# A two-layer float32 encoder on one core: x and the result kept with features on the partitions, and the first gate and up products alternating chunk by chunk

## The chip, the core and the metric

The kernel runs on one core of one Trainium2 chip. The metric is the device time of one execution in microseconds (us), taken as the median of 3 runs. Lower is better.

## The reference

An encoder of two layers works on x of 512 tokens by 1024 features, in float32. Each layer does three things:

- `x = x + 0.5 * swiglu(rms_norm(x))` with gate and up weights of 1024 x 2816 and a down weight of 2816 x 1024;
- `x = x + heads(rms_norm(x) @ w_in) @ w_out`, with four groups of attention heads;
- a second `x = x + 0.5 * swiglu(rms_norm(x))` with weights of its own.

`swiglu(h)` is `(silu(h @ w_gate) * (h @ w_up)) @ w_down`. The output is x after the second layer.

## The kernel before

TensorE multiplies float32 in halves: every operand is split into `hi` (rounded) and `lo` (the rest), and `mm3` (L237 to L240) issues three matmuls, hi by hi, hi by lo and lo by hi. ScalarE (ACT) makes `hi` as a cast on L190, VectorE (DVE) or GpSimd (POOL) makes `lo` on L191.

The residual stream lies on chip as eight tiles X[0..7], each of 128 features on the partitions by 512 tokens. XH and XL are its halves, scaled by the norm's gain. The norm's factor per token is not applied to them: products are made from the unscaled stream, and the factor R, spread over all partitions, multiplies each gate and up result when it leaves PSUM (L321, L325). So a gate product can begin before the sum of squares is known. The squares go through ACT and POOL into `acc`; `token_rstd` (L278) sums them on TensorE (L283), and `spread` (L294) makes R with one more matmul (L300).

A feed-forward block (`ffn`, L286) works on 22 column blocks of 128 in four groups (6, 6, 6 and 4). For a pair of columns the gate product (`wi` 0) and the up product (`wi` 1) each run over eight chunks of features, into two PSUM banks each. That is 8 chunks x 2 column blocks x 3 = 48 matmuls of 512 columns for the gate and 48 for the up. Then the down products of the group follow.

Weights come in blocks of 4 chunks by 256 columns (512 KB) through SP's DMA queue into three buffers `raw`, and are split two chunks at a time (a "piece") up to four pieces ahead of use (`run`, L193).

**The start.** x lies in memory as tokens by features, in the order of a 64-wide grid, while the kernel keeps tokens in blocks of 16 grid columns. So x comes in eight transfers `xin` (L849; four blocks of tokens, two halves of the features), each with a source of 8 x 16 rows of 2 KB. For each of the eight chunks, `begin` (L853) turns four 128 x 128 squares on TensorE (L867), which gives the chunk in PSUM; ACT makes XH (L868), DVE makes XL (L869) and copies X out (L874). The order of the first steps is written by hand (L412): four chunks, the first gate piece, two chunks, and so on. The gate runs its first four chunks, then the up its first four, then the gate its last four.

**The end.** The last group of the last block uses `row_products` (L368) instead of `down_products`: tokens on the partitions, 256 output columns to a matmul, 4 x 4 x 4 x 3 = 192 matmuls. For that `turn_rows` (L357) turns X back to tokens by features, with 32 more transposes on TensorE (L364) between the last up products. The result leaves in 16 transfers (L386) with a destination of 8 x 16 rows of 1 KB.

The names `psa`, `psb`, `psc` and `pso` are PSUM banks (2, 3, 2 and 1 of them). The order of work on each engine is the order in which the program writes it.

Of the kernel before, what the change touches and what calls it, by code (L numbers as in the profile page):

```python
# [10 lines left out]
F32 = mybir.dt.float32  # L11
# [14 lines left out]
# weight blocks being loaded, pieces of them held as halves, and pieces split ahead of the one in use  # L26
# [26 lines left out]
# those that stay on chip  # L53
# [3 lines left out]
def constants():  # L57
    """Tables and masks that depend on the shapes alone; the masks are for negated scores."""
# [10 lines left out]
    # tokens lie in blocks of 16 grid columns: (block, row, column)  # L69
# [22 lines left out]
    # windows of the grid's columns: row p is (grid row, column p % 16 of a block)  # L92
# [9 lines left out]
# the vectors of one layer that every partition holds: name -> (first column, columns)  # L102
# [21 lines left out]
def weave(mains, fills, ends):  # L124
    """Two streams of steps side by side: the part fills[i] is through when the share ends[i] of mains[i] is."""
# [21 lines left out]
def encoder(ctx: ExitStack, tc: tile.TileContext, a: dict, out: bass.AP):  # L147
# [45 lines left out]
    def run(steps):  # L193
        """Issue the steps, loading the weights and splitting them ahead of their use."""
        pieces = [x.src + (x.aside,) for x in steps if x.src]
        blocks = []
        for b, _, _ in pieces:
            if not blocks or blocks[-1] is not b:
                blocks.append(b)
        raws, ready = {}, []  # L200
        loaded = [0]

        def load(n):
            while loaded[0] < min(n, len(blocks)):
                b = blocks[loaded[0]]
                raw = raws[id(b)] = wp.tile([P, b.shape[1], b.shape[2]], F32, tag="raw", name="raw", bufs=RAW)
                nc.sync.dma_start(out=raw, in_=b)
                loaded[0] += 1

        fetch_x(0)  # L210
        load(1)
        fetch_x(1)
        load(RAW)
        used = at = 0
        for x in steps:
            used += x.src is not None
            while len(ready) < min(len(pieces), used + x.ahead):
                b, k, aside = pieces[len(ready)]
                if b is not blocks[at]:
                    # the block before is split: its place is free for another  # L220
                    at += 1
                    load(at + RAW)
                w = raws[id(b)][:, k:k + 2, :]
                hi, lo = (wp.tile([P, 2, b.shape[2]], F32R, tag=n, name=n, bufs=PIECES) for n in ("hi", "lo"))
                split(w, hi, lo, aside)
                ready.append((hi, lo))
            if x.src:
                x.go(ready[used - 1])
            else:
                x.go()  # L230

    def rows(w, r0, n, c0, m):
        """The pieces of n chunks of 128 rows and m columns: two chunks each."""
        b = w[r0 * P:(r0 + n) * P, c0:c0 + m].rearrange("(c p) f -> p c f", p=P)
        return [(b, k) for k in range(0, n, 2)]
# [6 lines left out]
    def feed(dc, g):  # L242
        """X[dc] is final: its scaled halves for the next products, and its squares."""
# [682 lines left out]
```

## Time and profile before

| | |
|---|---|
| runs | 2103.21, 2104.29, 2105.97 us; median 2104.29 us |
| profiled execution, first to last instruction | 2102.3 us |
| PE busy | 2043.9 us (97%), 10648 matmuls |
| PEld, DVE, ACT, POOL busy | 1689.5, 1067.8, 798.3, 408.1 us |
| read from memory, written | 176.56 MB, 2.10 MB (85 GB/s over the span) |

The profile states no time of its own for the profiled execution beside its span; the median of the runs is 2.0 us longer than the span. PE is TensorE, PEld its loads of the stationary operand, which overlap the matmuls. A matmul's shown duration includes its way through the array, so in a dense stretch the distance between two starts, not the duration, is what a matmul costs.

### The profile page before, as it was taken

Reading aid. Unit: us, or ns where it says so; the run is one execution under the profiler, and the core shown is the slowest. Engines: PE = TensorE matmul, PEld = TensorE weight load, DVE = VectorE, ACT = ScalarE, POOL = GpSimd, SP = SyncE. Lnnn points to the kernel's source line nnn. Section 1 sums busy time; section 2 is a strip of 40 time slices with the busy share of each in tenths; the row PEclk is TensorE's granted clock in tenths of the full one; section 3 lists DMA queues with packets and bytes.
Section 4 is the critical chain, followed back from the end, with each engine's and each line's share of the span. In section 5 each row is a group of like instructions: output and inputs, shape, how many; then the busy total and the mean of one; then the engine's idle time right before and its main releaser. Section 6 shows DMA issues by size and latency. Waiting matters only on the chain. (4 is left out here: it accounts for less than half of the span.)

```text
span 2102.3 us, 27434 instructions
## 1 busy us (share of the span) xinstructions
PE 2043.9 (97%) x10648; PEld 1689.5 (80%) x10648; DVE 1067.8 (51%) x1861; ACT 798.3 (38%) x1576; POOL 408.1 (19%) x403
## 2 busy tenths in 40 slices
PE   7999999999889999999999999999999899999998
PEld 5888888887767888888888888889887578888888
DVE  4444344757566543444454444455675664444444
ACT  4323222556554432332343322235565444232322
POOL 2000001364351200000110000033543511000100
PEclk9999999999989999999999999999999899999999
DMA  4333333321111323333333233333111123323232
GB/s 136 101 100 94 97 98 96 91 69 51 61 31 51 101 91 100 101 91 100 91 98 100 88 106 91 100 94 91 59 41 61 31 62 103 104 82 110 81 111 71
DMA packets 176514, 180.43 MB, mean 86 GB/s; under 512 B 6224, under 2 KB 174288, under 8 KB 176384
## 3 DMA queue, kind: packets, MB, share of 16 engines
q1 hardware_dynamic: 173632, 173.04, 27.5%
q0 software_dynamic: 1376, 4.50, 0.6%
q8 instruction: 83, 1.36, 0.3%
q10 hardware_dynamic: 1376, 1.14, 0.2%
q14 instruction: 47, 0.39, 0.1%
HBM read 176.56 MB, written 2.10 MB: 85 GB/s over the span
## 5 line engine op out<-in xcount | busy, mean ns | idle before, releaser
L190 ACT CAST hi<-raw 128x512 fp32r<-128x512 f32 x648 | 384.7, 618 | 488.3 <-PE pso L239 157.5
L191 DVE TENSOR_TENSOR lo<-raw,hi 128x512 fp32r<-128x512 f32 x566 | 392.5, 724 | 325.8 <-ACT hi L190 325.4
L326 POOL TENSOR_TENSOR u<-g,u 128x512 f32<-128x512 f32 x88 | 111.9, 1292 | 1225.7 <-DVE u L325 1225.7
L238 PE MATMUL psb<-XH,hi 128*128 128x512 f32 x556 | 217.4, 391 | 0.0
L239 PE MATMUL psb<-XL,hi 128*128 128x512 f32 x556 | 216.8, 390 | 0.0
L240 PE MATMUL psb<-XH,lo 128*128 128x512 f32 x556 | 216.8, 390 | 0.0
L191 POOL TENSOR_TENSOR lo<-raw,hi 128x512 fp32r<-128x512 f32 x82 | 112.4, 1380 | 240.6 <-ACT hi L190 236.5
L238 PE MATMUL psa<-hi,XH 128*128 128x256 f32 x512 | 154.8, 302 | 1.6 <-ACT qk L518 1.6
L238 PE MATMUL psa<-XH,hi 128*128 128x512 f32 x392 | 155.4, 396 | 0.0
L239 PE MATMUL psa<-XL,hi 128*128 128x512 f32 x392 | 153.2, 391 | 0.0
L240 PE MATMUL psa<-XH,lo 128*128 128x512 f32 x392 | 153.1, 391 | 0.0
L239 PE MATMUL psa<-lo,XH 128*128 128x256 f32 x512 | 144.4, 282 | 0.0
L240 PE MATMUL psa<-hi,XL 128*128 128x256 f32 x512 | 144.3, 282 | 0.0
L190 ACT CAST ph<-u 128x512 fp32r<-128x512 f32 x88 | 54.7, 622 | 228.5 <-POOL u L326 228.5
L322 ACT ACTIVATE g<-g 128x512 f32<-128x512 f32 x88 | 55.6, 632 | 206.3 <-DVE g L321 204.2
L238 PE MATMUL psc<-XH,hi 128*128 128x512 f32 x328 | 127.6, 389 | 0.0
L239 PE MATMUL psc<-XL,hi 128*128 128x512 f32 x328 | 127.6, 389 | 0.0
L240 PE MATMUL psc<-XH,lo 128*128 128x512 f32 x328 | 127.6, 389 | 0.0
L240 PEld LDWEIGHTS psb<-XH,lo 128*128 128x128 f32 x556 | 104.6, 188 | 21.8
L238 PEld LDWEIGHTS psb<-XH,hi 128*128 128x128 f32 x556 | 104.7, 188 | 21.6
L239 PEld LDWEIGHTS psb<-XL,hi 128*128 128x128 f32 x556 | 104.8, 188 | 21.5
L238 PEld LDWEIGHTS psa<-hi,XH 128*128 128x128 f32 x512 | 97.1, 190 | 23.7 <-issue 17.9
(226 smaller groups left out, 4339.8 us busy)
## 6 DMA issues: line engine op xcount, KB each, us to landing
raw<-in_ffn_w_gate_dram SPq DMA_DIRECT2D x88, 512.0 KB
raw<-in_ffn_w_up_dram SPq DMA_DIRECT2D x88, 512.0 KB
raw<-in_ffn_w_down_dram SPq DMA_DIRECT2D x64, 512.0 KB
raw<-in_w_in_dram SPq DMA_DIRECT2D x44, 512.0 KB
raw<-in_ffn_w_down_dram SPq DMA_DIRECT2D x48, 256.0 KB
raw<-in_w_out_dram SPq DMA_DIRECT2D x16, 512.0 KB
xin<-in_x_dram SPq DMA_DIRECT2D x8, 256.0 KB
dl<-in_consts_dram POOLq DMA_DIRECT2D x8, 256.0 KB, 4.6
```

The costliest lines, as they stand in the source:

```text
L190: nc.scalar.copy(hi, src)
L191: (nc.gpsimd if aside else nc.vector).tensor_tensor(out=lo, in0=src, in1=hi.bitcast(F32), op=ALU.subtract)
L238: nc.tensor.matmul(o, lh, rh, start=start, stop=False, skip_group_check=shared)
L239: nc.tensor.matmul(o, lh, rl, start=False, stop=False, skip_group_check=shared)
L240: nc.tensor.matmul(o, ll, rh, start=False, stop=stop, skip_group_check=shared)
L322: nc.scalar.activation(out=g, in_=g, func=AF.Silu)
L326: nc.gpsimd.tensor_tensor(out=u, in0=st["g", j], in1=u, op=ALU.mult)
```

## The change

The host hands x over as 1024 features by 512 tokens in the kernel's own order of tokens, and turns the result back. In the kernel:

- x comes straight into X, one transfer of 128 x 512 for each chunk. `begin` keeps only XH, XL and the squares, which now read X; the 32 transposes, the eight copies and the identity's own transfer are gone. The constants come in one transfer (POOL's queue, at chunk 5).
- The transfers of x and of the first four weight blocks are cut and interleaved: chunk 0 with gate and up chunk 0, chunk 1 likewise, then chunks by two. One of them goes through ACT's queue. The second and fourth block use buffers of the tag `pt`, which x no longer needs.
- In the first column pair the gate and up products alternate: gate chunk 0, up chunk 0, gate 1, up 1, gate 2 and 3, up 2 and 3, and so on. Their results leave PSUM (`finish_up`) only after `spread`, which now comes in the next pair's gate product.
- The last group uses `down_products` like all others: 96 matmuls of 512 columns. `turn_rows` and `row_products` are gone. The result leaves from X, in transfers of 128 x 512, the last two chunks in halves of 128 x 256.

The diff, cut to its core (blank lines that replace comments are left out):

```diff
-        fetch_x(0)
-        load(1)
-        fetch_x(1)
-        load(RAW)
...
+        firsts = [(b, place(b, ("raw", "pt")[i % 2])) for i, b in enumerate(blocks[:4])]
+        for c0, c1 in ((0, 1), (1, 2), (2, 4), (4, 6), (6, 8)):
+            for c in range(c0, c1):
+                nc.sync.dma_start(out=X[c], in_=a["x"][c * P:(c + 1) * P, :])
+            for i in range(2):
+                b, raw = firsts[2 * (c0 // 4) + i]
+                (nc.scalar if c0 == 0 and i == 0 else nc.sync).dma_start(out=raw[:, c0 % 4:c0 % 4 + c1 - c0, :], in_=b[:, c0 % 4:c0 % 4 + c1 - c0, :])
+        load()
...
-        vps = psum("c")
+        vps = psum("c" if preload else "b")
...
+                if first and fp == 0:
+                    st["late", wi] = lambda banks=st[wi]: finish_up(fp, wi, banks)
+                else:
+                    finish_up(fp, wi, st[wi])
...
+                end = last and final and dp == NDC - 2 and k0 + 2 == nf
+                order = [(k, j) for k in range(2) for j in range(2)]
+                for k, j in sorted(order, key=lambda kj: kj[1]) if end else order:
...
+                        if last and final:
+                            r = slice((dp + j) * P, (dp + j + 1) * P)
+                            for q in (slice(0, 256), slice(256, 512)) if dp == NDC - 2 else (slice(0, 512),):
+                                o = X[dp + j][:, q]
+                                nc.vector.scalar_tensor_tensor(
+                                    out=o, in0=st["d"][j][:, q], scalar=0.5, in1=o, op0=ALU.mult, op1=ALU.add)
+                                (nc.scalar if j else nc.sync).dma_start(out=out[r, q], in_=o)
+                            continue
...
-        def turn_rows(t, hf):
...
-        def row_products(f0, nf, c0, k0, src):
...
+                    if first and fp == 0:
+                        for k, n in ((0, 1), (1, 1), (2, 2)) if kb == 0 else ((0, 2), (2, 2)):
+                            steps += [up_products(fp, wi, kb + k, (src[wi][0][0], k, n)) for wi in range(2)]
...
-            return ([begin(dc) for dc in range(4)] + steps[:1] + [begin(4), begin(5)] + steps[1:2] + [begin(6), begin(7)] + steps[2:4] + [Step(0, rstd)] + steps[4:5] + [Step(0, spread)] + steps[5:])
+            return (b[:1] + steps[:1] + b[1:2] + steps[1:2] + b[2:4] + steps[2:4] + b[4:6] + steps[4:6] + b[6:] + steps[6:11]
+                    + [Step(0, rstd)] + steps[11:12] + [Step(0, spread), late] + steps[12:])
...
         def go():
             gc = gcol[:, 0, dc:dc + 1]
-            pt = psum("b" if dc < 3 else "c")
-            for t in range(4):
-                nc.tensor.transpose(pt[:, t * P:(t + 1) * P], xin[t][:, dc * P:(dc + 1) * P], ident)
-            nc.scalar.activation(out=XH[dc], in_=pt, func=AF.Copy, scale=gc)
...
+            nc.scalar.activation(out=XH[dc], in_=X[dc], func=AF.Copy, scale=gc)
...
+    given["x"] = np.ascontiguousarray(arr["x"][0].reshape(8, 4, 16, D).transpose(3, 1, 0, 2).reshape(D, S))
...
+    out = nc.dram_tensor("out_0_dram", (D, S), F32, kind="ExternalOutput").ap()
```

TensorE's order at the start of the program, before (`xin` are the x transfers' tiles, XH_84 and XH_85 the first two chunks, `hi` and `lo` the weight halves):

```order
L867 MATMUL psb<-cst,xin 128x128 x12
L867 MATMUL psc<-cst,xin 128x128 x4
L238 MATMUL psa<-XH_84,hi 128x512
L239 MATMUL psa<-XL_92,hi 128x512
L240 MATMUL psa<-XH_84,lo 128x512
L238 MATMUL psa<-XH_84,hi 128x512
L239 MATMUL psa<-XL_92,hi 128x512
L240 MATMUL psa<-XH_84,lo 128x512
L238 MATMUL psa<-XH_85,hi 128x512
```

And with the change (psa is the gate, psb the up):

```order
L250 MATMUL psa<-XH_84,hi 128x512
L251 MATMUL psa<-XL_92,hi 128x512
L252 MATMUL psa<-XH_84,lo 128x512
L250 MATMUL psa<-XH_84,hi 128x512
L251 MATMUL psa<-XL_92,hi 128x512
L252 MATMUL psa<-XH_84,lo 128x512
L250 MATMUL psb<-XH_84,hi 128x512
L251 MATMUL psb<-XL_92,hi 128x512
L252 MATMUL psb<-XH_84,lo 128x512
L250 MATMUL psb<-XH_84,hi 128x512
L251 MATMUL psb<-XL_92,hi 128x512
L252 MATMUL psb<-XH_84,lo 128x512
```

Sixteen transposes stood ahead of the first product and sixteen more between products; now the first product is the first instruction, and chunk 0 serves twelve matmuls instead of six before chunk 1 is wanted.

SP's DMA queue at the start, before:

```order
L849 DMA xin<-in_x_dram 128x1x512 x4
L207 DMA raw<-in_ffn_w_gate_dram 128x4x256
L849 DMA xin<-in_x_dram 128x1x512
L849 DMA xin<-in_x_dram 128x1x512 [waits DMAHW0_49]
L849 DMA xin<-in_x_dram 128x1x512 [waits DMAHW1_49]
L849 DMA xin<-in_x_dram 128x1x512 [waits DMAHW2_49]
L207 DMA raw<-in_ffn_w_up_dram 128x4x256 [waits DMAHW3_49]
L207 DMA raw<-in_ffn_w_gate_dram 128x4x256 [waits DMAHW4_49]
```

And with the change (raw_107 is the up block in a `pt` buffer; a DMAHW semaphore is that of an earlier transfer, eight back):

```order
L220 DMA X_76<-in_x_dram 128x512
L223 DMA raw_107<-in_ffn_w_up_dram 128x256
L220 DMA X_77<-in_x_dram 128x512
L223 DMA raw<-in_ffn_w_gate_dram 128x256
L223 DMA raw_107<-in_ffn_w_up_dram 128x256
L220 DMA X_78<-in_x_dram 128x512
L220 DMA X_79<-in_x_dram 128x512 [waits DMAHW0_49]
L223 DMA raw<-in_ffn_w_gate_dram 128x2x256 [waits DMAHW1_49]
L223 DMA raw_107<-in_ffn_w_up_dram 128x2x256 [waits DMAHW2_49]
L220 DMA X_80<-in_x_dram 128x512 [waits DMAHW3_49]
L220 DMA X_81<-in_x_dram 128x512 [waits DMAHW4_49]
L223 DMA raw<-in_ffn_w_gate_dram 128x2x256 [waits DMAHW5_49]
```

Half of all features of every token had to come before the first chunk could be turned; now the first chunk is one transfer, and 17 transfers on SP's queue and one on ACT's carry what 12 carried on SP's.

TensorE's order where the norm's factor is spread, with the change (psc is the second column pair's gate, pso_385 the spread factor, psb_413 and pso_414 the second pair's up; the sums of squares stand twelve matmuls earlier):

```order
L250 MATMUL psc_338<-XH3_87,hi_281 128x512
L251 MATMUL psc_338<-XL3_95,hi_281 128x512
L252 MATMUL psc_338<-XH3_87,lo_282 128x512
L312 MATMUL pso_385<-dg_383,ones_75 128x512
L250 MATMUL psb_413<-XH0_84,hi_299 128x512
L251 MATMUL psb_413<-XL0_92,hi_299 128x512
L252 MATMUL psb_413<-XH0_84,lo_300 128x512
L250 MATMUL pso_414<-XH0_84,hi_299 128x512
```

Before, both stood inside the first pair (after its up product's fourth chunk and its gate product's sixth); now the sums come after the 108th product of the program and the spread after the 120th, and pso_414 waits for ACT to have copied the factor out of pso_385.

## Rows read from the trace of the kernel before

**Rows 1.** The page's first part: span, and busy time, share of the span and instructions of the engines.

```profile
span 2102.3 us, 27434 instructions
PE 2043.9 (97%) x10648; PEld 1689.5 (80%) x10648; DVE 1067.8 (51%) x1861; ACT 798.3 (38%) x1576; POOL 408.1 (19%) x403
```

**Rows 2.** What PE waited for in the whole span: us in total, times, longest us.

```profile
PE psb L867 <- DMA xin<-in_x_dram: 9.5, 4, 5.2
PE psc L867 <- DVE X L874: 2.9, 2, 2.3
PE psc L867 <- DMA xin<-in_x_dram: 1.4, 1, 1.4
```

**Rows 3.** Busy time by stretch, from the start to the 121st gate or up matmul: length, busy us of PE, PEld, DVE, ACT, POOL (instructions), granted clock, share of the DMA engines, GB/s.

```profile
0.00:13.59 13.59, 4.11 (x17) 3.24 (x17) 1.52 (x3) 3.29 (x5) 0.20 (x4) 1.00 0.66 173
13.59:34.43 20.84, 16.52 (x66) 12.77 (x64) 13.56 (x21) 11.81 (x21) 12.98 (x10) 0.92 0.64 180
34.43:52.81 18.38, 18.38 (x84) 14.90 (x83) 9.51 (x17) 8.41 (x15) 2.54 (x2) 1.00 0.20 58
```

**Rows 4.** The timeline of the start: start us, duration us, engine, line, operation, and in brackets the idle time before it and what ended it.

```profile
0.74 2.77 SPq L849 DMA_DIRECT2D xin<-in_x_dram  x4
...
5.16 0.47 PE L867 MATMUL psb<-cst,xin 128*128 128x128 f32 x1 [5.16 <-DMA xin<-in_x_dram]
...
10.90 2.18 PE L867 MATMUL psb<-cst,xin 128*128 128x128 f32 x9 [1.46 <-DMA xin<-in_x_dram]
...
12.27 0.69 ACT L868 ACTIVATE XH<-psb,gcol 128x512 fp32r<-128x512 f32 x1 [0.17 <-PE psb L867]
...
12.85 0.62 ACT L190 CAST hi<-raw 128x512 fp32r<-128x512 f32 x1
...
13.59 0.78 PE L238 MATMUL psa<-XH,hi 128*128 128x512 f32 x1
...
17.04 0.40 PE L240 MATMUL psa<-XH,lo 128*128 128x512 f32 x1
...
20.10 0.77 PE L867 MATMUL psc<-cst,xin 128*128 128x128 f32 x5 [1.41 <-DMA xin<-in_x_dram]
...
20.94 0.40 PE L239 MATMUL psa<-XL,hi 128*128 128x512 f32 x1
...
22.75 0.62 ACT L190 CAST hi<-raw 128x512 fp32r<-128x512 f32 x1 [0.29 <-DMA raw<-in_ffn_w_gate_dram]
...
27.85 0.78 PE L238 MATMUL psb<-XH,hi 128*128 128x512 f32 x1
...
30.55 0.40 PE L238 MATMUL psb<-XH,hi 128*128 128x512 f32 x1
...
52.81 0.39 PE L238 MATMUL psb<-XH,hi 128*128 128x512 f32 x1
...
54.17 0.39 PE L238 MATMUL psb<-XH,hi 128*128 128x512 f32 x1
```

**Rows 5.** The timeline around the norm's factor: the last product ahead of the sums of squares and the first behind them, the products around the spread (L300), and ACT's copy of it.

```profile
34.43 0.39 PE L240 MATMUL psb<-XH,lo 128*128 128x512 f32 x1
...
35.46 0.49 PE L238 MATMUL psa<-XH,hi 128*128 128x512 f32 x1
...
38.10 0.39 PE L240 MATMUL psa<-XH,lo 128*128 128x512 f32 x1
38.33 1.02 PE L300 MATMUL pso<-dg,ones 128*128 128x512 f32 x2
...
39.39 0.59 ACT L302 COPY R<-pso 128x512 f32<-128x512 f32 x1 [2.60 <-PE pso L300]
...
39.42 0.40 PE L239 MATMUL psa<-XL,hi 128*128 128x512 f32 x1
```

**Rows 6.** Busy time by stretch, columns as in rows 3, at three places: only x transfers of the start in flight; a single weight block in flight; only transfers of the result in flight.

```profile
3.00:4.00 1.00, 0.00 (x0) 0.00 (x0) 0.00 (x0) 0.00 (x0) 0.00 (x0) 1.00 0.56 192
...
43.50:44.00 0.50, 0.50 (x4) 0.40 (x3) 0.00 (x0) 0.50 (x3) 0.00 (x0) 1.00 1.10 381
...
2098.00:2098.50 0.50, 0.00 (x0) 0.00 (x0) 0.00 (x0) 0.00 (x0) 0.00 (x0) 1.00 0.56 195
```

**Rows 7.** The page's costliest groups: DVE's share of the split (count, busy us, mean ns, idle before).

```profile
L191 DVE TENSOR_TENSOR lo<-raw,hi 128x512 fp32r<-128x512 f32 x566 | 392.5, 724 | 325.8 <-ACT hi L190 325.4
```

**Rows 8.** The timeline around the first of the four places where `turn_rows` stands, with eight transposes between the first and the second row.

```profile
2049.82 0.39 PE L240 MATMUL psa<-XH,lo 128*128 128x512 f32 x1
...
2050.84 0.47 PE L238 MATMUL psa<-XH,hi 128*128 128x512 f32 x1
...
2051.16 0.40 PE L239 MATMUL psa<-XL,hi 128*128 128x512 f32 x1
```

**Rows 9.** The timeline of the last product: its first and its last matmul, of 192, and DVE's last two instructions.

```profile
2072.69 0.28 PE L238 MATMUL psc<-hi,ph 128*128 128x256 f32 x1
...
2096.59 0.28 PE L240 MATMUL psb<-hi,pl 128*128 128x256 f32 x1
2096.91 0.76 DVE L384 SCALAR_TENSOR_TENSOR o<-psb,xtok 128x256 f32<-128x256 f32 x2 [0.68 <-PE psb L240]
```

**Rows 10.** SP's time to issue a transfer: those of the result (ns, smallest, median and largest, first and last start), and one weight block.

```profile
L386 SPq DMA_DIRECT2D out_dram<-o x8: 603/603/666, 2079.0 to 2097.7; - x8
...
41.25 0.37 SPq L207 DMA_DIRECT2D raw<-in_ffn_w_up_dram  x1
```

More of the change, by code (lines that the diff above doesn't have):

```diff
@@ L195, in run, with place, load @@
         pieces = [x.src + (x.aside,) for x in steps if x.src]
-        blocks = []
-        for b, _, _ in pieces:
-            if not blocks or blocks[-1] is not b:
+        blocks, left = [], {}
+        for b, _, _, _ in pieces:
+            if id(b) not in left:
                 blocks.append(b)
+            left[id(b)] = left.get(id(b), 0) + 1
         raws, ready = {}, []
-        loaded = [0]
-        def load(n):
-            while loaded[0] < min(n, len(blocks)):
-                b = blocks[loaded[0]]
-                raw = raws[id(b)] = wp.tile([P, b.shape[1], b.shape[2]], F32, tag="raw", name="raw", bufs=RAW)
-                nc.sync.dma_start(out=raw, in_=b)
-                loaded[0] += 1
-        fetch_x(0)
-        load(1)
-        fetch_x(1)
-        load(RAW)
-        used = at = 0
+        loaded, held = [0], [0]
+        def place(b, tag="raw"):
+            raws[id(b)] = wp.tile([P, b.shape[1], b.shape[2]], F32, tag="raw", name="raw", bufs=RAW) if tag == "raw" else \
+                tp.tile([P, 4, 256], F32, tag="pt", name="raw0", bufs=4)
+            loaded[0] += 1
+            held[0] += tag == "raw"
+            return raws[id(b)]
+        def load():
+            while loaded[0] < len(blocks) and held[0] < RAW:
+                b = blocks[loaded[0]]
+                nc.sync.dma_start(out=place(b), in_=b)
+        firsts = [(b, place(b, ("raw", "pt")[i % 2])) for i, b in enumerate(blocks[:4])]
[6 more added lines that the diff above has]
+        load()
+        used = 0
         for x in steps:
@@ L217, in run @@
             while len(ready) < min(len(pieces), used + x.ahead):
[L218 to L224, printed above, removed]
+                b, k, n, aside = pieces[len(ready)]
+                w = raws[id(b)][:, k:k + n, :]
+                hi, lo = (wp.tile([P, 2, b.shape[2]], F32R, tag=z, name=z, bufs=PIECES)[:, :n, :] for z in ("hi", "lo"))
                 split(w, hi, lo, aside)
                 ready.append((hi, lo))
+                left[id(b)] -= 1
+                if left[id(b)] == 0:
+                    held[0] -= all(b is not blocks[i] for i in (1, 3))
+                    load()
             if x.src:
@@ L234, in rows @@
         b = w[r0 * P:(r0 + n) * P, c0:c0 + m].rearrange("(c p) f -> p c f", p=P)
-        return [(b, k) for k in range(0, n, 2)]
+        return [(b, k, 2) for k in range(0, n, 2)]
     def mm3(o, lh, ll, rh, rl, start, stop, shared=False):
@@ L310, in go @@
                     st[wi] = two_banks()
-                for k in range(2):
+                for k in range(src[2]):
                     kc = k0 + k
@@ L338, in go @@
                 hi, lo = w
-                if final and dp == k0 == 0 and g_next % 3 == 1:
+                if final and not last and dp == k0 == 0 and g_next % 3 == 1:
                     pairs[0] = 1
@@ L409, in ffn @@
[L409 to L412 removed]
+                    src = [rows((wg, wu)[wi], kb, 4, fp * P, 256) for wi in range(2)]
+                    if first and fp == 0:
+                        for k, n in ((0, 1), (1, 1), (2, 2)) if kb == 0 else ((0, 2), (2, 2)):
+                            steps += [up_products(fp, wi, kb + k, (src[wi][0][0], k, n)) for wi in range(2)]
+                    else:
+                        steps += [up_products(fp, wi, kb + 2 * i, src[wi][i]) for wi in range(2) for i in range(2)]
@@ new lines, in ffn @@
+            final = gi == len(groups) - 1
+            for dp in range(0, NDC, 2):
+                src = rows(wd, f0, 4, dp * P, 256) + (rows(wd, f0 + 4, 2, dp * P, 256) if nf == 6 else [])
+                steps += [down_products(f0, nf, dp, k0, final, src[k0 // 2]) for k0 in range(0, nf, 2)]
+        if first:
+            for x, n in zip(steps, (1, 2, 1, 2, 2, 3, 3)):
+                x.ahead = n
+            b = [begin(dc) for dc in range(NDC)]
+            late = Step(0, lambda: [st["late", wi]() for wi in range(2)])
+            return (b[:1] + steps[:1] + b[1:2] + steps[1:2] + b[2:4] + steps[2:4] + b[4:6] + steps[4:6] + b[6:] + steps[6:11]
+                    + [Step(0, rstd)] + steps[11:12] + [Step(0, spread), late] + steps[12:])
```

117 lines of the change are left out of this document (29 added, 88 removed).

## The prediction

> **What bounds the kernel now.** I read the page's first part, then PE's waits, then the busy time by stretch and the timeline of both ends. The first part says that PE is busy 97% of the span [rows 1], so only time on PE's path counts, and 58 us of the span are not covered. The waits show that the largest stalls that have to do with x lie at the start: 9.5 us until x transfers land, and 4.3 us more between transposes [rows 2]. The stretches show how badly the start runs: 4.1 us of work in the first 13.6 us, 16.5 in the next 20.8, and full from 34.43 on [rows 3]. The steady price of a gate or up matmul is the distance of two starts: six of them from 52.81 to 54.17, so 0.2267 us each [rows 4]. The matmul at 52.81 is the 121st gate or up product: 120 x 0.2267 = 27.2 us of work took 52.8 us. What is not full in the start and at the end is what the change can move; the 2000 us between have the same instructions in the same order.
>
> **The start, step by step.** I follow the changed program to its own 121st product.
>
> *First product.* Today the first x transfer, issued at 0.74, lets PE begin at 5.16, and the first real product stands at 13.59 [rows 4]. In the change chunk 0 is one x transfer of 262 KB, two weight pieces of 131 KB and the small gains, 0.55 MB; by 5.16 the old queue had landed 0.35 MB. While only x is in flight the DMA engines are 0.56 busy and move 192 GB/s, against 1.10 and 381 GB/s for a weight block [rows 6], and the new x transfers have the weight block's form, 128 rows on 128 partitions. At twice the rate the 0.55 MB need about as long as the 0.35 MB did, so I let x land at 5.16. Behind it stands one XH, 0.69 us [rows 4]; the gate cast of half width runs next on ACT, under way while PE starts, so 5.85 us for the first product. Bounds: 4.5, with x alone at twice the rate (0.262 MB in 0.69 instead of 1.37 us), and 10.9, where PE got today's fourth x transfer [rows 4], if the first ones are held up by those issued behind them as they are today.
>
> *Clock.* Today's first products run slowly: eight spacings from 13.59 to 17.04 take 3.45 us instead of 1.81, and six from 27.85 to 30.55 take 2.70 instead of 1.36 [rows 4]. [...] I take 1.64 us once, since the first product now comes cold and no pause follows; bounds 1.34, and 2.8, if the slow time counts from PE's first transpose at 10.90 to 17.04, 14 products at 0.2 us extra.
>
> *Transfers.* 4.19 MB (2.10 of x, 2.10 of weights) must land for the first pair. Today 3.67 MB (2.10 of x and three blocks) had landed at 22.75, when ACT got the block it waited for [rows 4]: 22.0 us from the first issue, 0.167 MB/us. At that rate the last new piece lands at 25.9; with its cast, 0.62 us [rows 4], and split, 0.72 [rows 7], it is ready at 27.2. PE reaches it after 84 products, at 5.85 + 84 x 0.2267 + 1.64 = 26.5. So even at the old rate the wait is 0.7 us; at the weight block's rate there is none. I take 0. At the end far off stands today's first half of x: 1.05 MB in 10.2 us up to 10.90 [rows 4], 0.103 MB/us, with which the last piece is ready at 42.8, 16.3 us late. I choose the near end, because the 3.67 MB are nearly the same bytes in the same queue. The queue itself now holds 17 issues for x and the first blocks at 0.37 us each [rows 10], 6.3 us; each waits for the one eight before it, so SP may stand, but the DMA engines have seven others meanwhile. The third block's use frees no buffer late: the next blocks are asked for only from the 97th product on.
>
> *Other engines.* Two chunks cost ACT two XH, two squares and two casts, under 4 us at 0.62 to 0.69 [rows 4], and DVE less, beside 5.44 us of PE. The vanished eight copies and transposes save them nothing that PE waits for otherwise. POOL's transfer of the constants stands ahead of its additions for chunks 4 to 7; it is wanted only at the spread, some 15 us later.
>
> *Sums and spread.* The sums of squares keep PE 35.46 - 34.43 - 0.23 = 0.80 us, the spread 39.42 - 38.10 - 2 x 0.2267 = 0.87 us [rows 5]; both stay. New is that pso is wanted four matmuls behind the spread: today ACT's copy ends 1.65 us after the spread's start (39.98 against 38.33) and the fourth product would come at 1.55. I charge 0.1 us. The late evacuation of the first pair is covered: its four banks are wanted again 48 products later, 10.9 us. If it were not, four DVE passes of 0.7 us would show.
>
> Sum: 5.85 + 27.2 + 1.64 + 0.80 + 0.87 + 0.1 = 36.4 against 52.81. **The start gives 16.4 us.**
>
> **The end.** *Transposes.* A group of eight costs 2050.84 - 2049.82 - 0.23 = 0.79, and 0.09 more in the next spacing [rows 8]; four groups: 3.5 us, wholly on PE's path. *Last product.* 192 matmuls take 2096.59 - 2072.69 + 0.12 = 24.0 us [rows 9]; 96 of 512 columns take 21.8. The old ones stood about 1 us for the halves of the last hidden columns (192 x 0.12 is 23.0). The new ones want them after 12 matmuls, 2.72 us, instead of 24, 2.88 us, so I charge 0.55 and get 22.3: 1.7 us. *Drain.* From the end of PE's work at 2096.7 to 2102.3 are 5.6 us: DVE to 2097.67 [rows 9], an issue of 0.60 to 0.67 [rows 10], transfers at 0.56 of the engines [rows 6], landing. The new transfers have 128 rows on 128 partitions. If they issue like a weight block (0.37) and move 0.26 MB behind PE's end at twice the rate, 1.3 us go (0.25 and about 1); if only the issue changes, 0.25. I take 1.3, the block's form being theirs. Sum: **6.5 us.**
>
> [...]
>
> **Forecast.** 16.4 + 6.5 = 22.9 us off the profiled span of 2102.3 gives 2079.4; the median of the runs stands 2.0 above that span, so 2081.4 us. Its own range is 2079 (first product at 4.5, clock 1.34, a shorter drain) to 2085 (clock 2.8, no faster drain, 0.7 us of transfers).
>
> **Rivals.**
>
> *Transfers become the bound of the start.* Every product of the first pair waits for its chunk. For it: the slow first half of x, 0.103 MB/us. Against it: 0.167 over the whole, and the half-used engines. With the far rate 16.3 us go: 2097.7; with 0.13 MB/us the last piece is ready at 34.3, 7.8 us late: 2089.
>
> *The first chunk lands late*, because seven transfers share the engines with it: first product at 10.9, 5 us more: 2086.5.
>
> *The clock stays low through the first pair.* [...] All 96: 19.2 - 1.6 = 17.6 us: 2099. For it: pauses for chunks, as at 27.85, where little but transposes had run for 4 us. Against it: after the wait that ended at 20.10 the products run at full distance (0.40 us of duration at 20.94) [rows 4], and the new order pauses less. [...]
>
> *Slower than before.* The same mechanism goes on past the first pair, with PE's pauses for each piece as cause, so that the three pairs of the first group, 288 products, run low: 57.6 - 1.6 = 56 us: 2137. It decides from 8 + 22.9 / 0.2 = 122 slow products on. Against it: from 34.43 on PE never pauses with the DMA engines a fifth busy [rows 3].
>
> *The change does not do what it says*: x arrives chunk by chunk, but the first products still begin near 13.6. Then the start gives what the missing gaps between give, some 8 us, and the end 6.5: 2090.
>
> **How the numbers follow.** Forecast 0.68, late first chunk 0.08, transfers 0.13, late start 0.02, low clock 0.05, slower 0.02, no net change 0.02. A measurement of this kernel can tell about 0.2%, 4.2 us: all but the last two cases are faster, and I add a little to "same" for the far ends: faster 0.95, same 0.03, slower 0.02. The range, 2078.5 to 2090, holds the forecast's own range, the late chunk and the near half of the transfers' case; the far transfers, the low clock and the losses stay outside.
>
> **What would show it.** Right: the first product near 6 us, products of gate and up alternating with no wait above 1 us up to the 96th near 29.3, the 121st near 36.4, x transfers in flight with the engines well above 0.56; no gap of eight transposes near the end; 96 products of 512 columns at 0.227; 4.3 us from PE's last work to the span's end. Wrong: PE waiting for ACT's casts that wait for a DMA (transfers), spacings of 0.43 us beyond the first eight or so (clock), a wait of more than 2 us behind the spread (banks).

## The result, and the profile after

The changed kernel takes 2081.66 us (median; 2080.21 to 2082.88) against 2103.75 (2102.86 to 2105.97) before on the same chip: a ratio of 0.9897, 95% interval 0.9883 to 0.991, 22.1 us less. The profiled execution took 2082.88 us in all, 1.8 more than its span.

The page's first part, as in [rows 1]:

```profile
span 2081.1 us, 27083 instructions
PE 2032.8 (98%) x10488; PEld 1677.0 (81%) x10488; DVE 1066.5 (51%) x1847; ACT 796.3 (38%) x1574; POOL 406.0 (20%) x401
```

What PE waited for in the first 40 us (us, times, longest), where [rows 2] had 13.8 us:

```profile
PE psa L250 <- ACT hi L190: 5.1, 1, 5.1
```

Busy time in the stretch of the first of [rows 6], columns as in [rows 3]. x and the first weight pieces are in flight together here, and move at the share and rate that a weight block has there:

```profile
3.00:4.00 1.00, 0.00 (x0) 0.00 (x0) 0.00 (x0) 0.00 (x0) 0.00 (x0) 1.00 1.09 375
```

SP's issue of the first pair's last transfer, and how long that transfer took to land (the last number, us). So the pair's 4.19 MB were there at 15.7 us:

```profile
9.96 0.38 SPq L223 DMA_DIRECT2D raw<-in_ffn_w_up_dram  x1
```

```profile
raw<-in_ffn_w_up_dram SPq DMA_DIRECT2D x1, 256.0 KB, 5.7
```

The timeline of the start, as [rows 4 and 5]: the first XH, the first product, the 10th and 11th, the spread, the 121st product (psb) and the 124th (pso):

```profile
4.03 0.72 ACT L850 ACTIVATE XH<-X,gcol 128x512 fp32r<-128x512 f32 x1 [2.01 <-DMA gcol<-in_gains_dram]
...
5.10 0.80 PE L250 MATMUL psa<-XH,hi 128*128 128x512 f32 x1 [5.10 <-ACT hi L190]
...
9.17 0.44 PE L250 MATMUL psb<-XH,hi 128*128 128x512 f32 x1
...
9.46 0.40 PE L251 MATMUL psb<-XL,hi 128*128 128x512 f32 x1
...
35.35 1.02 PE L312 MATMUL pso<-dg,ones 128*128 128x512 f32 x2
35.81 0.79 PE L250 MATMUL psb<-XH,hi 128*128 128x512 f32 x1
...
37.05 0.50 PE L250 MATMUL pso<-XH,hi 128*128 128x512 f32 x1
```

The 124th product before, not among the rows above:

```profile
53.49 0.39 PE L238 MATMUL pso<-XH,hi 128*128 128x512 f32 x1
```

The end, as [rows 9]: the first of the last product's 96 matmuls, the one stall in it, the last matmul, DVE's last work and the last issues:

```profile
2054.59 0.39 PE L250 MATMUL psc<-ph,hi 128*128 128x512 f32 x1
...
2057.31 0.39 PE L250 MATMUL psc<-ph,hi 128*128 128x512 f32 x1
...
2058.11 0.50 PE L251 MATMUL psc<-pl,hi 128*128 128x512 f32 x1 [0.42 <-DVE pl L191]
...
2076.88 0.39 PE L252 MATMUL psb<-ph,lo 128*128 128x512 f32 x1
2077.30 0.76 DVE L376 SCALAR_TENSOR_TENSOR X<-psb,X 128x256 f32<-128x256 f32 x2 [0.61 <-PE psb L252]
2077.76 0.82 ACTq L378 DMA_DIRECT2D out_dram<-X  x2
```

Busy time while the last of the result is in flight, as the last of [rows 6]:

```profile
2079.00:2079.50 0.50, 0.00 (x0) 0.00 (x0) 0.00 (x0) 0.00 (x0) 0.00 (x0) 1.00 0.79 268
```

Four segments add up to the spans' difference of 21.2 us. Start, to the 124th product: 53.49 - 37.05 = 16.4. From there to the last product's first matmul: 2019.2 against 2017.5, 1.7. Last product: 24.0 against 2076.88 - 2054.59 + 0.23 = 22.5, so 1.5. Drain: 5.6 against 4.0, so 1.6. The second segment should have given the transposes' 3.5; the experiment `again` finds the missing 1.8.

### The profile page after: what moved, and what is told of

It is laid out like the page before. It is cut to its first block, busy times and chain, and to the rows that moved or that the text cites. A ratio compares the mean times of both kernels' runs of the same rounds, so it can differ in the third digit from the quotient of the medians.

```text
span 2081.1 us, 27083 instructions
## 1 busy us (share of the span) xinstructions
PE 2032.8 (98%) x10488; PEld 1677.0 (81%) x10488; DVE 1066.5 (51%) x1847; ACT 796.3 (38%) x1574; POOL 406.0 (20%) x401
## 5 line engine op out<-in xcount | busy, mean ns | idle before, releaser
L190 ACT CAST hi<-raw 128x512 fp32r<-128x512 f32 (+1 forms) x650 | 384.8, 617 | 489.8 <-PE psb L251 160.0
L191 DVE TENSOR_TENSOR lo<-raw,hi 128x512 fp32r<-128x512 f32 (+1 forms) x570 | 393.3, 722 | 314.7 <-ACT hi L190 314.4
L252 PEld LDWEIGHTS psb<-XH,lo 128*128 128x128 f32 x556 | 104.4, 188 | 21.9
```

The source lines that it names most:

```text
L190: nc.scalar.copy(hi, src)
L191: (nc.gpsimd if aside else nc.vector).tensor_tensor(out=lo, in0=src, in1=hi.bitcast(F32), op=ALU.subtract)
L252: nc.tensor.matmul(o, ll, rh, start=False, stop=stop, skip_group_check=shared)
```

## Experiments

Times are medians. Kernels that ran together share runs of the kernel before: 2103.47 us for start_only, end_only, gate_first and half_engines; 2103.06 for again, warm, warm_late and gate_first_late; 2103.71 for gate_first_sums, fill and fill_tail; 2103.56 for gate_first_idle_pool.

### The two ends apart: start_only and end_only

start_only is the changed kernel with `turn_rows`, `row_products` and the old result layout back; end_only is the kernel before with only the new end.

```diff
+            if last and final:
+                for i in range(8):
+                    steps.insert(len(steps) - 7 + i // 2, turn_rows(i // 2, i % 2))
+            if last and final:
+                for c0 in range(0, D, 256):
+                    src = rows(wd, f0, nf, c0, 256)
+                    steps += [row_products(f0, nf, c0, k0, src[k0 // 2]) for k0 in range(0, nf, 2)]
+            else:
```

The lines are start_only's; end_only takes the same ones away.

> The changed start with the old end (transposes, row products and 16 result transfers as before). Theory, start and end are separate sums: the 121st gate or up product stands at 35.8 us as in the changed kernel, 16.3 us of the 22 are there, so about 2087.4 us against 2103.75 before; the last transpose group, last product and drain are those of before (24.0 and 5.6 us). Rival, the new start costs 1.8 us again at the attention of layer 0, near 380 us, whatever the clock does: 2089.2, and the profile shows the same 1.8 us of distance lost there with PE at its full clock. Rival, the end's gain needs the start or the other way round: below 14 or above 18 us.

> The old start with the changed end (X evacuated as features by tokens, 96 products of 512 columns, result transfers of 128 rows). Theory: 6.7 us, of which the four groups of transposes 3.5, the last product 1.5 to 1.7, the drain 1.3 to 1.6, so about 2097.1 us against 2103.75; the 121st product stands at 52.8 as before. Rival, the transposes were hidden behind the wait for the last hidden columns: 3.2 us, 2100.5.

Measured: start_only 2088.22 (ratio 0.9926, 0.9911 to 0.9941), 15.25 less than before; end_only 2096.78 (0.9967, 0.9954 to 0.998), 6.7 less. Together 21.9 of 22.1: two separate sums. The transposes were not hidden: the rival's 3.2 us lies outside end_only's interval, which is 4.2 to 9.7 us. start_only's rival of 1.8 us near 380 us wanted PE at its full clock there. Its profile does lose 1.5 us between the 124th product and the last product's first matmul; the changed kernel's first profile loses 1.8 us there, with the granted clock at 0.50 from 384 to 388, and `again` settles this.

### Where 1.8 us went in the middle: again

The changed kernel unaltered, profiled once more.

> The changed kernel once more, for another profile of it: its first one lost 1.8 us against before between 380 and 390 us, in a half-clock stretch of 6.8 us where before had one of 3.4. Theory, the length of that stretch depends on where the run's clock steps fall against the work and not on the kernel: span 2079.3 if the stretch is 3.4 us long this time, 2081.1 if 6.8; the 124th product at 37.0 plus or minus 0.5 in either case. Rival, the change itself costs 1.8 us there: then the same distance is lost with PE at its full clock. Median 2081.5.

Measured: 2081.42 (0.9897, 0.988 to 0.9913), span 2078.9. The clock column (last but two), first profile and then this one:

```profile
380.00:384.00 4.00, 3.20 (x17) 3.21 (x18) 3.39 (x10) 3.18 (x7) 0.74 (x1) 0.67 0.20 38
384.00:388.00 4.00, 4.00 (x21) 4.00 (x21) 1.18 (x2) 1.90 (x5) 0.00 (x0) 0.50 0.70 225
```

```profile
380.00:384.00 4.00, 3.10 (x18) 3.10 (x19) 3.39 (x10) 3.28 (x7) 0.85 (x1) 0.74 0.20 52
384.00:388.00 4.00, 4.00 (x31) 4.00 (x30) 1.28 (x2) 2.91 (x6) 0.00 (x0) 0.84 0.65 210
```

In 384 to 388 PE issues 21 matmuls at a granted clock of 0.50 and 31 at 0.84. The 124th product and the end of this second profile:

```profile
37.20 0.50 PE L250 MATMUL pso<-XH,hi 128*128 128x512 f32 x1
...
2052.43 0.39 PE L250 MATMUL psc<-ph,hi 128*128 128x512 f32 x1
...
2074.71 0.39 PE L252 MATMUL psb<-ph,lo 128*128 128x512 f32 x1
```

Its segments: 16.3, then 2019.2 - 2015.2 = 4.0, then 1.5 and 1.6. So the same kernel has the longer fall in one run and the shorter in another. Eight more profiles with the new end agree: from the 124th product to the last matmul it is 2037.4 to 2038.1 us in end_only, warm and the four gate_first kernels, like the 2037.5 of `again`, and 2039.2 to 2039.8 in half_engines and warm_late, like the 2039.8 of the first profile. It is the run, not the change.

### The alternation: gate_first, gate_first_late, gate_first_sums, gate_first_idle_pool

gate_first takes the alternation back and nothing else (with it the number of pieces split ahead of the first steps):

```diff
+                        m = 6 if kb == 0 else 4
+                        steps[-m:] = steps[-m::2] + steps[1 - m::2]
...
-            for x, n in zip(steps, (1, 2, 1, 2, 2, 3, 3)):
+            for x, n in zip(steps, (0, 0, 0, 0, 1, 2, 3)):
```

> The changed kernel with one thing undone: in the first column pair the gate product runs its first four chunks, then the up product its first four, then both their last four, as before; layout and transfers of x stay, in the same queue order. Theory, the layout and the whole-width transfers carry the start: a chunk of x with its two weight pieces (0.52 MB) lands every 1.45 us at 0.36 MB/us and would now be wanted every 1.36 us, so only the third and fourth chunk come late, 0.5 to 1.5 us in all: 2082.7 us against 2081.66 for the changed kernel; the 121st product at 36.3 to 37.3. Rival, the alternation carries the start: PE waits at each of the chunks and its clock falls with the pauses, 5 us or more: 2087 or above, the 121st product beyond 41.

Measured: 2084.52 (0.9908, 0.9892 to 0.9925), 2.9 above the changed kernel: between the two expectations. The 121st product stands at 39.97. PE's waits in the first 45 us:

```profile
PE psa L250 <- ACT hi L190: 5.9, 2, 4.9
PE psb L252 <- DVE lo L191: 1.4, 1, 1.4
PE psa L252 <- DVE lo L191: 1.3, 1, 1.3
```

None ends with a DMA: DVE and ACT, not transfers, are late. DVE's XL in this kernel (count: smallest, median and largest ns, first and last start):

```profile
L853 DVE SCALAR_TENSOR_TENSOR XL<-X,gcol,XH x8: 739/750/2331, 4.6 to 22.6; 128x512 fp32r<-128x512 f32 x8
```

And its timeline, POOL and DVE alone:

```profile
8.71 4.72 POOL L848 TENSOR_TENSOR acc<-acc,sq 128x512 f32<-128x512 f32 x3 [8.26 <-ACT sq L847]
...
9.28 1.31 DVE L853 SCALAR_TENSOR_TENSOR XL<-X,gcol,XH 128x512 fp32r<-128x512 f32 x1 [0.38 <-ACT XH L852]
...
10.51 3.20 DVE L191 TENSOR_TENSOR lo<-raw,hi 128x512 fp32r<-128x512 f32 x2
```

Beside POOL's additions DVE's XL takes up to 2331 ns where its smallest is 739, and the two lo take 3.20 us where one takes 0.69 in the median of the kernel before. The next three kernels take work away from there. gate_first_late puts squares and sums behind all chunks, as steps `q`:

```diff
-            for c in {0: (), NDC - 1: (NDC - 2, NDC - 1)}.get(dc, (dc - 1,)):
-                square(c)
-        return Step(0, go, ahead=0)
+        return Step(0, go, ahead=0), Step(0, lambda: square(dc), ahead=0)
...
+ b[6:] + steps[6:8] + q[:4] + steps[8:10] + q[4:] + steps[10:11]
```

gate_first_sums leaves the squares and puts the additions into a later step `sums`; gate_first_idle_pool does that with the first square ahead of them, and moves the constants to SP's queue:

```diff
-                nc.scalar.activation(out=acc, in_=X[c], func=AF.Square)
+                return
...
+    def sums():
+        nc.scalar.activation(out=acc, in_=X[0], func=AF.Square)
+        for c in range(1, NDC):
+            nc.gpsimd.tensor_tensor(out=acc, in0=acc, in1=sqs[c], op=ALU.add)
...
-                nc.gpsimd.dma_start(out=cst, in_=a["consts"][:, 0:C_STAY])
+                nc.sync.dma_start(out=cst, in_=a["consts"][:, 0:C_STAY])
```

> The kernel gate_first with the squares of x (ACT) and their sums (POOL) put behind all eight chunks of the first pair, products and transfers as in gate_first. There PE waited 4.8 us between products for ACT's and DVE's halves, with ACT without a pause and DVE's XL and lo at 1.3 to 1.6 us instead of 0.75 while POOL added squares. Theory, the making of halves bounds the start without the alternation, and the squares slow it on both engines: the waits fall to 0.5 to 1.5 us, the 121st product from 39.97 to about 36.5, 2081.6 to 2082.5 us; DVE's XL at 0.75. Rival, the transfers bound it: the waits stay within 1 us of 4.8, 2084.5. A wait for POOL's sum behind the 108th product would be a cost of moving the squares and not of either theory.

> The kernel gate_first with POOL's seven additions of squares alone put behind all eight chunks (the squares wait in buffers that stand idle); ACT's squares stay at their place. It parts the two engines that gate_first_late relieved together. Theory, POOL slows DVE: XL from x in SBUF reads two operands there and took up to 2.05 us beside POOL's additions, where before it read PSUM and took 0.74 to 0.75; with the additions gone XL and lo are back at 0.75, the two waits for DVE's lo in gate_first (1.4 and 1.5 us) go, the one for ACT's cast (1.2 us at 10.3) stays: waits of 1.0 to 2.0 us in all, 121st product at 37.3 to 38, about 2082.9 us. Rival, ACT's squares are what delays the halves: waits of 3.5 us or more remain, 39 or later, 2084.

> The kernel gate_first with POOL kept out of the first pair by a data dependence, since moving its additions in the program alone (gate_first_sums) left them where they were: the square of chunk 0, with which the sum begins, is made by ACT behind the seven others, which wait in idle buffers; the constants go through SP's queue behind the first blocks. ACT does the same work, but for that one square. Theory, POOL's additions slow DVE: XL and lo are at 0.75 and 0.68 us until about 19 us, the two waits for lo (1.4 and 1.5 us) go and a wait of at most 1.2 us for ACT's cast stays: waits of 0.5 to 1.5 us between products, 121st product at 36.5 to 37.5, 2082.7 us. Rival, ACT's squares delay the halves: DVE's 0.75 changes nothing, since DVE waits for ACT; waits of 3 us or more, 39 or later, 2084.5.

gate_first_late: 2082.65 (0.99, 0.9885 to 0.9915). No wait at all between products; the 121st at 36.36.

gate_first_sums failed as an experiment: 2084.91 (0.9915, 0.9899 to 0.9932), and POOL's first addition began at 9.90. POOL had nothing else to do there, so the addition, written later in the program, still started 0.07 us behind its square's end at 9.83. It says nothing on the question.

gate_first_idle_pool: 2083.28 (0.9907, 0.989 to 0.9923), with ACT's squares of chunks 1 to 7 in place. DVE's XL:

```profile
L859 DVE SCALAR_TENSOR_TENSOR XL<-X,gcol,XH x8: 750/752/752, 4.7 to 17.2; 128x512 fp32r<-128x512 f32 x8
```

All that PE waited for in the first 45 us:

```profile
PE psa L250 <- ACT hi L190: 5.0, 1, 5.0
```

The 121st product is at 36.47. So POOL's additions cost gate_first its two waits for DVE. The wait for ACT is another matter. ACT's casts and the 13th product, first in gate_first, then here:

```profile
9.67 0.91 ACT L190 CAST hi<-raw 128x512 fp32r<-128x512 f32 x2
...
10.32 0.50 PE L250 MATMUL psa<-XH,hi 128*128 128x512 f32 x1 [1.01 <-ACT hi L190]
```

```profile
9.51 0.91 ACT L190 CAST hi<-raw 128x512 fp32r<-128x512 f32 x2
...
10.38 0.55 PE L250 MATMUL psa<-XH,hi 128*128 128x512 f32 x1
```

The casts stand only 0.16 us apart. What differs is PE: its products reach full distance at 8.0 us in gate_first and at 10.8 here, so there it came early and waited, and here it came late and did not. From the 13th to the 121st product gate_first takes 29.65 us, this kernel 26.09 and the changed kernel 25.89: with POOL idle the old order of products is as good as the new behind the 13th. The medians of gate_first_late and gate_first_idle_pool stay 1.0 and 1.6 us above the changed kernel's, but their runs overlap with its runs. The trace of before has the contrast inside one kernel:

```profile
22.02 1.29 POOL L191 TENSOR_TENSOR lo<-raw,hi 128x512 fp32r<-128x512 f32 x1 [2.65 <-ACT hi L190]
22.49 1.97 DVE L191 TENSOR_TENSOR lo<-raw,hi 128x512 fp32r<-128x512 f32 x2 [3.75 <-ACT hi L190]
...
27.88 1.66 POOL L861 TENSOR_TENSOR acc<-acc,sq 128x512 f32<-128x512 f32 x1 [0.64 <-ACT sq L860]
28.31 0.74 DVE L869 SCALAR_TENSOR_TENSOR XL<-psc,gcol,XH 128x512 fp32r<-128x512 f32 x1
```

Beside POOL's lo the first of DVE's two lo, both operands of which lie on chip in SBUF, took 1.36 us (two in 1.97 instead of 1.3), and it ended at 23.86, 0.55 us behind POOL's end at 23.31; the second took 0.68. XL, one operand of which lay in PSUM, took 0.74 beside POOL's addition, and 0.74 to 0.75 in all eight chunks. Not every lo beside POOL took longer: one that began at 29.57, 0.04 us ahead of a POOL addition, took 0.68, and that addition 1.78 instead of 1.26. The change moved XL's operand from PSUM to X in SBUF, and in the changed kernel the eight XL take 0.75 to 2.05 us. Why the one delays the other, no run shows.

### The transfers' form: half_engines

The changed kernel, with x and the result padded in memory to 8 groups of 17 rows, so that a transfer's far side is 8 x 16 rows again:

```diff
-                nc.sync.dma_start(out=X[c], in_=a["x"][c * P:(c + 1) * P, :])
+                nc.sync.dma_start(out=X[c], in_=a["x"][c, :, 0:16, :])
-                                (nc.scalar if j else nc.sync).dma_start(out=out[r, q], in_=o)
+                                (nc.scalar if j else nc.sync).dma_start(out=out[dp + j, :, 0:16, q], in_=o)
```

> The changed kernel with x and the result lying in memory as 8 groups of 16 rows with a gap behind each group, so that their transfers have a side of 8 x 16 rows as before; all else as in the changed kernel. Theory, the form with 8 halves the engines of a transfer: x alone at about 190 GB/s, first product 0.5 us later (5.6), no wait for transfers after it, since 2.10 MB of x at half the engines and half of the weights there are 16.5 us against 24 us of products; result transfers at a share near 0.5, drain 1.0 us longer (5.0 against 4.0); 2083.2 us. Rival, the half rate belonged to the old order of x's rows and not to the form: share near 1.0 at both ends, 2081.7. Rival, x becomes the bound at half rate: products wait chunk by chunk, 5 us or more: 2087.

Measured: 2087.43 (0.9923, 0.9908 to 0.9937), 5.8 above the changed kernel. Two stretches (in the first, weight pieces are in flight beside x), and the first product and last issues:

```profile
3.00:4.00 1.00, 0.00 (x0) 0.00 (x0) 0.00 (x0) 0.00 (x0) 0.00 (x0) 1.00 0.77 169
2083.00:2083.50 0.50, 0.00 (x0) 0.00 (x0) 0.00 (x0) 0.00 (x0) 0.00 (x0) 1.00 0.54 184
```

```profile
6.78 0.79 PE L250 MATMUL psa<-XH,hi 128*128 128x512 f32 x1 [6.78 <-ACT hi L190]
...
2080.66 1.32 ACTq L377 DMA_DIRECT2D out_dram<-X  x2
```

Here the form sets the rate: 184 GB/s at 0.54 for the result instead of 268 at 0.79, an issue 0.66 instead of 0.41 us. At both ends the old form brings the lower rate back: 169 GB/s at 0.77 instead of 375 at 1.09 in the first stretch, and 184 at 0.54 in the last, where before had 195 at 0.56 [rows 6]. The size was nearly four times my expectation, 5.8 instead of 1.5 us: the first product comes 1.7 us later, not 0.5, with XH waiting for x until 5.71 instead of 4.03 (why so much more, no run shows); twelve products instead of nine are slow; a wait at the 27th product costs 0.9; in all 3.5 us at the 124th. The drain is 1.6 us longer, all that the change had gained there.

### The clock: warm, warm_late, fill, fill_tail

warm, ahead of the program's steps:

```diff
+    nc.vector.memset(XL[NDC - 1].bitcast(F32), 0.0)
+    dummy = psum("o")
+    for i in range(8):
+        nc.tensor.matmul(dummy, XL[NDC - 1][:, 0:P], XL[NDC - 1], start=True, stop=True)
```

warm_late has the squares late besides, and sends the last piece of the result through SP's queue.

> The changed kernel with eight matmuls of 512 columns on zeros ahead of the first product, into a bank that nobody reads, from 1.4 to 4.9 us, while PE waits for x. Theory, the clock of the first products depends on what PE did before them: in the changed kernel nine spacings from 5.10 to 9.17 take 4.07 us instead of 2.04; with the zeros ahead at most three of them are slow and 1.4 to 2.0 us go from there, of which 0.3 to 0.8 come back as waits for the third and fourth chunk (their halves are ready at 10.3 to 11 us and would now be wanted at 10.5): 121st product at 34.6, 2080.5 us. Rival, the slow products belong to the first us of the program whatever PE did before: 121st product at 35.8, 2081.7. Rival, the chunks bound the start as soon as the clock does not: all of it comes back as waits, 35.8 as well, but with full distances and gaps between.

> The kernel warm with the squares moved behind the chunks' halves too, and the last 128x256 of the result through SP's queue instead of ACT's. Theory: no waits for chunks behind the warm first products, 121st product at 34.0, and the last issue starts 0.4 us earlier, so 2.1 us less than the changed kernel: 2079.6 us. Rival, squares and chunks do not meet in this order: the same as warm. Rival, POOL's sum comes too late for the sums of squares behind the 108th product: a wait there of up to 2 us, 2081.5.

warm: 2080.59 (0.9893, 0.9878 to 0.9907); warm_late: 2081.08 (0.9892, 0.9877 to 0.9907); neither can be told from the changed kernel. warm's start:

```profile
1.46 3.78 PE L840 MATMUL pso<-XL 128*128 128x512 f32 x8 [1.46 <-DVE XL L836]
5.04 0.68 PE L250 MATMUL psa<-XH,hi 128*128 128x512 f32 x1
...
7.24 0.39 PE L252 MATMUL psa<-XH,lo 128*128 128x512 f32 x1
...
12.52 0.50 PE L252 MATMUL psa<-XH,lo 128*128 128x512 f32 x1 [0.32 <-DVE lo L191]
```

Full distances begin at 7.24 instead of 9.46, in warm_late at 6.22. Without the zeros the place differs by run: in seven other profiles whose first product stands at 4.9 to 5.1 us and that do not wait in the first eight products, it lies between 8.0 and 10.8. Both kernels with zeros are earlier than all of these, so in these runs the slow first distances do depend on what PE did before. Five slow spacings instead of ten save 1.0 us, and 0.6 comes back at 12.52, where PE waits for DVE: the 121st product stands at 35.42, 0.4 earlier. In warm_late it stands at 35.30; what took the rest there is not shown.

fill, in `token_rstd`, with 12 for the mixers' sums and 0 elsewhere; fill_tail has a like loop in `turn` besides:

```diff
+        for i in range(fill):
+            nc.tensor.matmul(vps, XH[0][:, 0:P], XH[0], start=True, stop=True)
```

> The changed kernel with twelve matmuls of 512 columns ahead of the sums of squares of both mixers, into the bank of those sums, which overwrite it. PE waits there 2.85 us for POOL (377.9 to 380.9 in the last profile of the changed kernel) and its clock falls behind the pause; 12 x 0.2267 = 2.72 us fit into it. Theory, the pause makes the fall: without it no half-clock stretch at 380 to 390 us nor at the same place in layer 1, which cost 1.7 us each where they last 3.4 us and 3.4 us each where they last 6.8: 3.4 to 6.8 us, 2076.5 us (2075 to 2078.3) against 2081.5; the spread between runs narrows. Rival, the fall comes from the load of the products ahead of the pause (down products, power) and not from the pause: same stretches, 2081.5, or 2082.5 where the twelve delay the sums.

> The kernel fill with further matmuls of 512 columns, 8, 5 and 2 of them, ahead of the last three transpositions of the last group of heads in each layer, where PE waited 2.0, 1.3 and 0.65 us for probabilities; a half-clock stretch of about 13.7 us began some 11 us behind the first of these waits. Theory, as in fill: the stretch goes or begins later, and of its 13.7 us at half rate the busy part comes back, 2 to 5 us in each layer: 2070 us (2066 to 2074). Rival, the chain of softmax on DVE and ACT bounds that stretch and the clock costs nothing there: as fill, or some tenths slower for matmuls that overrun their wait.

fill: **2077.59 (0.9877, 0.9863 to 0.9892), faster than both kernels**; its four runs (2076.93 to 2077.87) lie below all eight of the changed kernel (2080.21 to 2082.88). The sums of squares in `again`, then in fill, and fill's clock at that place:

```profile
380.90 0.83 PE L295 MATMUL psc<-ones,acc 128*128 128x1 f32 x6 [2.85 <-POOL acc L264]
```

```profile
377.85 2.91 PE L295 MATMUL psc<-XH 128*128 128x512 f32 x12
380.93 0.72 PE L297 MATMUL psc<-ones,acc 128*128 128x1 f32 x5 [0.17 <-POOL acc L264]
```

```profile
380.00:384.00 4.00, 3.83 (x30) 3.37 (x29) 3.39 (x10) 3.43 (x8) 0.88 (x1) 1.00 0.17 45
384.00:388.00 4.00, 4.00 (x36) 4.00 (x35) 2.17 (x5) 2.86 (x7) 0.00 (x0) 1.00 0.69 217
```

The sums start when they did, and the fall is gone: 36 matmuls instead of 21 or 31. One pause of 2.85 us made it. In layer 1 `again` has a pause of 2.86 us up to 1414.65, and behind it, from 1416.31 to 1419.30, products of 256 columns 0.21 us apart instead of 0.12; fill has its other twelve matmuls there, the last near 1412.8, and what stands behind them is not shown. The mean granted clock is 0.994 in all four runs of fill and 0.991 to 0.993 in the eight of the changed kernel.

fill_tail: 2084.60 (0.9911, 0.9897 to 0.9926), slower than fill by 7.0. Its matmuls stood in the wrong place:

```profile
L703 PE MATMUL psc<-XH x30: 389/389/504, 643.0 to 1689.3; 128*128 128x512 f32 x30
```

The waits meant lie near 584 to 597, in the third group of heads, not the last; at 643 PE had no wait to fill, and 30 x 0.2267 = 6.8 us were simply added. Whether the longer fall there (0.50 from 596 to 600 in `again`) costs anything stays untried.

## Why the prediction was right, point by point

The forecast was 2081.4 and the result 2081.66; the gain was put at 22.9 us and is 22.1 between medians. By its terms:

*First product*, put at 5.85, came at 5.10. Transfers of chunk 0 were faster than the 5.16 that I let x have: XH starts at 4.03, and it waited last for the gains. The gate cast, which I let run beside PE's start, stood on the path: PE waited for it, and began 0.35 us behind XH's end at 4.75. The lower bound of 4.5 had left XH out; 5.85 less the 0.68 that x alone can save is 5.2. *Clock*, put at 1.64: the first ten spacings, 5.10 to 9.46, take 4.36 instead of 2.27 us, so 2.1, a little of it XL; by run these ten take 3.8 to 4.5 us in the profiles without zeros that start at 4.9 to 5.1 and do not wait among them. (In the prediction's upper bound, 10.90 is PE's fourth transpose; the first stands at 5.16 [rows 4].) The clock column shows 1.00 from 5.10 to 9.46; only the distances tell. The 0.2 us that the rivals on the clock charge for each slow product, 19.2 for the 96 of the first pair, is the spacing of [rows 4], 3.45 / 8 = 0.43, less 0.2267. *The rest up to the 121st product*: 110 x 0.2267 = 24.9 of 26.35, so 1.4 for sums and spread where 0.80 + 0.87 were put. Together 35.81 against 36.4, and after the spread 0.4 and 0.15 are lost behind the 121st. At the 124th: 16.4, the figure forecast; the errors, -0.75, +0.45, -0.3 and +0.5, cancel, so the agreement to a tenth is luck. Of the 16.4 us, half_engines shows 3.5 to hang on the transfers' form, and gate_first 4.2 (39.97 against 35.81) on the alternation beside POOL's additions. How the rest divides between the missing transposes, the arrival chunk by chunk and the interleaved weights, no run parts.

*Transfers 0*: right, with room. All was there at 15.7 us, not 25.9: 4.19 MB in 14.9 us from the first issue are 0.28 MB/us instead of 0.167. The rival in which they bound the start was further off than its 0.13.

*Other engines*: here the working was thin. It put two chunks at under 4 us of ACT "and DVE less". DVE's two XL of chunks 4 and 5 alone:

```profile
12.52 3.76 DVE L851 SCALAR_TENSOR_TENSOR XL<-X,gcol,XH 128x512 fp32r<-128x512 f32 x2
```

With two lo of 0.68 that is 5.1 of the 5.44 us that PE takes, and for chunks 6 and 7, where one lo also takes 1.78, it is 5.8 us (17.41 to 23.20), more than PE takes. What covered it was the lead that DVE had by then, since the alternation wants a new chunk only every twelve products: with six PE waits (gate_first). I had not seen that XL would now read two operands from SBUF beside POOL. Most of the price of the old order, 2.9 us, is this and not the transfers: with POOL idle (gate_first_idle_pool) the 121st product comes 3.5 us earlier than in gate_first.

*Transposes* 3.5, *last product* 1.7, *drain* 1.3: end_only gives 6.7 for the three. The last product is 22.5 instead of 22.3, with 0.57 lost at 2057.31 where 0.55 was put; the drain gives 1.6. That the new transfers would move at the block's rate because they have its form was an estimate of mine from [rows 6]. Its "about 1" for the transfers was no result of the rows: 0.26 MB at 195 and at 381 GB/s differ by 0.7. half_engines shows the drain's gain to be the transfers' form alone, with 1.7 of the 8.5 us by which the first product comes earlier.

*The 2000 us between* were put at no change. The instructions are the same, yet the first profile lost 1.8 us there and the second gained about 0.5 over the transposes: a fall of the clock behind a pause, longer or shorter by run (0.50 and 0.84 granted from 384 to 388). A term for that, of either sign, was missing.

## What to carry to other kernels

Count the operands of each VectorE instruction that a change moves from PSUM to SBUF, and look at what GpSimd does beside it: here the two XL of chunks 4 and 5, 1.5 us undisturbed, took 3.76. Before filling or hiding anything, read which wait stands where; twelve idle matmuls in each of two pauses of 2.85 us gave 4 us, and thirty without a pause cost 7. And writing POOL's additions later in the program did not hold them back while its queue was empty (the first began at 9.90, 0.07 us behind its square): give such an engine an operand that comes late.

## What was not expected of the hardware

- VectorE's XL, 128x512 float32, took 0.75 us undisturbed (gate_first_idle_pool) and up to 2.3 beside GpSimd's additions (gate_first), when both its operands lay in SBUF.
- One pause of TensorE of 2.85 us (`again`), in an otherwise full stretch, was followed by a stretch of lower granted clock (0.84 from 384 to 388, 0.50 in the first profile) that cost 1.7 to 3.4 us (what the clock column lacks of 1.00, times the length), differently from run to run of one kernel.
- Issuing a transfer of the result through ACT's queue took 0.66 us with 8 x 16 rows on one side (half_engines) and 0.41 with 128 rows (the changed kernel).
